# A memory operand gated in other tiles, branch sums moved to VectorE, and a reordered end of an attention stage

## The chip, the cores and the metric

The kernel runs on one core of one Trainium2 chip. A core has TensorE for matrix products (PE in the profile, with PEld for its weight loads), VectorE (DVE), ScalarE (ACT), GpSimd (POOL), and SyncE (SP), whose queue issues most transfers (DMAs) between HBM and the on-chip memory, SBUF. Products land in PSUM, eight banks of 128 x 512 float32. The metric is the time of one execution in microseconds; lower is better.

## The reference, cut to what matters

The kernel computes one encoder block: a normalised input is projected, three mixers run side by side (dilated window attention `oa`, grouped attention `ob`, attention into a fixed memory `om`), each is gated, projected and merged, and one output projection follows.

```python
ya = (oa * jax.nn.silu(ga)) @ w_br_a[layer]
yb = (ob * jax.nn.silu(gb)) @ w_br_b[layer]
ym = (om * jax.nn.silu(gm)) @ w_br_m[layer]
gates = jax.nn.sigmoid((mg + b_merge[layer]).astype(jnp.float32)).astype(dt).reshape(b, s, N_BRANCHES, d)
merged = gates[:, :, 0] * ya + gates[:, :, 1] * yb + gates[:, :, 2] * ym
out = merged @ w_out[layer]
x = x + rms_norm(out, g_post[layer])
```

The sequence has 1024 tokens and the model is 1024 wide; a branch is 512 wide, that is four blocks of 128 channels. Everything is float32: each factor of a product is split into a high part in a reduced format and a low part, and each product is three passes (high x high, high x low, low x high). The helper `split` does it with one ScalarE copy (L105) and one VectorE subtraction (L106).

## The kernel before, in words

All tiles are 128 partitions by 512 or 1024 columns. PE's instructions stand in the order in which the code emits them, and from the value stage on the orders of ACT, DVE, POOL and SP are those of the code too. An engine that waits for one instruction holds back everything behind it; SP's queue does the same with the transfers that it issues.

Three stages matter here.

**The values of head group 0** (the second loop `for n in range(28)`, L1271; PE's line is L1281). Large products are cut in two by two and computed with seven products (Strassen's scheme), `PRODUCTS`: A11, A12, S2, S3, S4, S1, A22. Product i takes the steps n = 4i to 4i+3, twelve 256-column matmuls a step. Its weights must have been summed (`v3_sum`) and split (`v3_split`, into two buffers each of `wh` and `wl`) before step 4i. Results come out through `v3_evac` (DVE additions on L1196) one or two steps after a product's last, and are scaled (ACT L1185, DVE L1183) and stored (SP L1186) by `v3_out`. The dictionary `SIDE` says what else the other engines are given after the matmuls of step n: the splits (S2 at 4, S3 at 8, S4 at 12, S1 at 16, A22 at 20), the token splits `kt_split`, the loads of the next stage's weights (`k_load`), the next stage's first weight sums and splits (`k_sum` on POOL, `k_own` and `k_block` on ACT and DVE, steps 23 to 27), and three strands of interest:

- `operand(r, stage)` (L982) finishes block r of the grouped branch's operand: load its output, its gate and its reciprocals, multiply twice on DVE (L992, L993), store (L995). Stages 1 and 2 of r = 7, the last, stand at steps 2 and 3.
- `memory_operand(k, stage)` (L997) gates block k of the memory branch, 128 x 1024, in two halves: stage 0 loads output and gate into the four half tiles vot, vot, vgt, vrt that `operand` uses too (SP L1003, four transfers of 256 KB), stage 1 multiplies (DVE L1007, twice), stage 2 stores the halves (SP L1011). Block j has its stages at steps 3+3j, 5+3j and 6+3j, none later than 14.
- `tab[0]` and `tab[1]` (L1289) are two 128 x 1024 tiles with the cosines and sines by which the next stage turns queries and keys. They are loaded at step 9 (SP L1258) and multiplied by the row norms at step 11 (`tab[1]`, POOL) and step 17 (`tab[0]`, DVE), both on L1259.

**The query, key, gate and merge products** follow at once (`pair_product`, PE line L1320): for each of 25 pairs the same seven products, in the order A11, A12, S2, S1, S3, A11 of the next pair, A22, and so on. The first needs the tiles of `k_own(0)`, the third, fourth and fifth those of `k_block(0, ...)` for S2, S1 and S3. The merge products' sigmoids, as tanh, go to DRAM (`thd`).

**The window attention with the branch projections beside it** (`weave`, L176, called on L1980). Sixteen items `add_y(m)` (L1864; PE line L1879) are projections of the memory branch (m 0 to 7) and the grouped branch (m 8 to 15), 24 matmuls each in two halves. `weave` alternates them with the steps of the attention by estimated costs: it advances the attention whenever its share of `att_cost` is not above the projections' share. An item puts small jobs on the list `pend`, from which one is taken at every third matmul: `th_load(m+1)` loads the item's gate into one of two wl tiles, `y_load(m+2)` its weights into one of two wr tiles, `y_split(m+1, G)` splits the weights (ACT L1353, POOL L1354), and after each half `y_evac` (L1363). For m below 8 `y_evac` starts the sum `accs`; from 8 on it writes (gate + 1) x product over the gate tile (DVE L1371) and adds that to `accs` (L1372), on POOL below m = 16 and on DVE from there. The last attention pieces come from `ending()` (L1968): small weights are spread over the rows by PE (`wide`), and `first_two(x)` sums two of three terms for column half x. `third(x)` (L1961) adds the third, reading its factor from PSUM, and multiplies by the gate: three DVE operations, L1964 to L1966. `dl_high` (ACT L1859) and `dl_low` (DVE L1862 for block 3) split the result, which is block 3 of the last operand.

After the weave (L1981 on) the code empties `pend`, splits the weights of projections 17 and 18 (`y_split` on ACT L1353 and DVE L1354), loads those of 19 and the first output weights, and then runs `third` and the splits of both halves. The last eight projections (m 16 to 23, PE line L2023) follow: m 16, 17 and 18 first with operand blocks 0 and 1, then with block 2, then with block 3. Their products are tiles of two PSUM banks, three of them, in the place of the weave's six banks. The output products (L2105) end the kernel.

Of the kernel before, what the change touches and what calls it, by code (L numbers as in the profile page):

```python
# [16 lines left out]
NT = 8  # L17
# [33 lines left out]
def block(ctx: ExitStack, tc: tile.TileContext, x, xT, memT, cst, msk, bcst, tabA, gpost,  # L51
# [945 lines left out]
    def memory_operand(k, stage):  # L997

        if stage == 0:
            OT["m"] = [vb.tile([P, 512], F32, name=x, bufs=2 if x == "vot" else 1) for x in ("vot", "vot", "vgt", "vrt")]  # L1000
            for z in range(2):
                for src, dst in ((od, OT["m"][z]), (g2d, OT["m"][2 + z])):
                    nc.sync.dma_start(dst, src[2, k, :, half[z]])  # L1003
        elif stage == 1:
            for z in range(2):
                o, g = OT["m"][z::2]
                V.scalar_tensor_tensor(o, o, 0.5, g, op0=OP.mult, op1=OP.mult)  # L1007
        else:
            o = OT.pop("m")
            for z in range(2):  # L1010
                nc.sync.dma_start(od[2, k, :, half[z]], o[z])  # L1011
# [161 lines left out]
    def v3_split(nm):  # L1173
        h, l = wslot(0), wslot(1)
        split(h, l, V3[nm])
        W3[nm] = [z.rearrange("p (k f) -> p k f", k=4) for z in (h, l)]
# [41 lines left out]
    for n in range(28):  # L1218
# [34 lines left out]
        if k == 3:  # L1253
# [4 lines left out]
            8: [lambda: v3_split("S3")], 9: [lambda: [nc.sync.dma_start(tab[j], tabA[:, j]) for j in range(2)]],  # L1258
            11: [lambda: G.tensor_tensor(tab[1], tab[1], rb, op=OP.mult)], 17: [lambda: V.tensor_tensor(tab[0], tab[0], rb, op=OP.mult)],  # L1259
# [5 lines left out]
    SIDE[2].append(lambda: operand(7, 1))  # L1265
    SIDE.setdefault(3, []).append(lambda: operand(7, 2))
    for j in range(4):
        for z in range(3):
            at = min(3 + 3 * j + (0, 2, 3)[z], 14)
            SIDE.setdefault(at, []).append(lambda j=j, z=z: memory_operand(j, z))  # L1270
# [92 lines left out]
    def y_evac(m, t, ps_):  # L1363
        n, i, f = steps[m]
        th = THS[m]
        if n == 0:
            if accs[f] is None:
                accs[f] = hp.tile([P, S], F32, name=f"acc{f}", tag=f"{('hh', 'hl')[f // 4]}{4 + f % 4}")
            V.scalar_tensor_tensor(accs[f][:, t], th[:, t], 1.0, ps_, op0=OP.add, op1=OP.mult)
        else:  # L1370
            V.scalar_tensor_tensor(th[:, t], th[:, t], 1.0, ps_, op0=OP.add, op1=OP.mult)  # L1371
            (V if m >= 16 else G).tensor_tensor(accs[f][:, t], accs[f][:, t], th[:, t], op=OP.add)  # L1372
# [106 lines left out]
    with ExitStack():  # L1479
# [378 lines left out]
        def dl_high(k, t=slice(0, S)):  # L1858
            A.activation(hh[k][:, t], DL[k][:, t], AF.Copy)  # L1859
# [4 lines left out]
        def add_y(m):  # L1864
            n, i, f = steps[m]

            def gen(_):
                pend.extend([lambda: th_load(m + 1), lambda: y_load(m + 2)])
                if m:
                    pend.append(lambda: y_split(m + 1, G))  # L1870
                if m == 15:
                    pend.append(lambda: y_load(18))
                for t in half:
# [94 lines left out]
        def ending():  # L1968
            DL[3] = C["ogs"][0]
            return [(lambda: [wide(g, 0) for g in range(2)], 500.0), (lambda: [wide(g, 1) for g in range(2)], 500.0),  # L1970
                    (lambda: [first_two(0), wide(2, 0)], 2500.0), (lambda: [first_two(1), wide(2, 1)], 2500.0)]
# [8 lines left out]
        weave(16, every(), FIRST_PAD + 12 * NT * (SOFT + 100.0) + 4 * LAST_PAD + 8000.0)  # L1980
        while pend:  # L1981
            pend.pop(0)()
        y_split(17)
        y_split(18, V, qk.tile([P, S], R, name="aq", bufs=2))
# [5 lines left out]
        third(0)  # L1990
        dl_high(3, lo)
        third(1)
        dl_low(3, lo)
        dl_high(3, hi)
        dl_low(3, hi)
# [340 lines left out]
```

## Time and profile before

| what | us |
|---|---|
| median of 3 runs | 1445.68 |
| lowest, highest | 1442.84, 1447.82 |
| the profiled execution's own time | 1446.26 |
| its span, first to last instruction | 1444.5 |

The profiled execution lies 0.58 us above the median, and 1.76 us of it lie around the span. The page lists, engine by engine, busy time, a strip of 40 slices with the TensorE clock that was granted, the chain of work that ended last, and the costliest groups of instructions. Views of the trace behind it give the instructions in order of time (start, duration, engine, line, operands, and in brackets the idle time before and what ended it), who waited for whom, and busy times by stretch. Times in them count from the span's start.

### The profile page before, as it was taken

The numbers are of one execution on the slowest core, as the hardware profiler recorded it, in microseconds if no ns is written. First come the engines' busy times: TensorE is split into PE (matmuls) and PEld (weight loads), VectorE is DVE, ScalarE is ACT, GpSimd is POOL, SyncE is SP. The second block draws the span as 40 slices with busy tenths as digits, with TensorE's granted clock in tenths as the row PEclk, the third lists the DMA queues.
The fourth block names the chain that finished last, engine by engine and source line by source line (L and its number), as shares of the span: only waits on it lengthen the run. The fifth ranks groups of instructions, "written<-read, shape, count | busy, mean of one in ns | idle before, by whom it ended". The sixth has DMA issues, their size and how long they took to land.

```text
span 1444.5 us, 21871 instructions
## 1 busy us (share of the span) xinstructions
PE 1392.9 (96%) x7775; PEld 1112.6 (77%) x7775; DVE 1012.0 (70%) x1811; ACT 659.6 (46%) x1384; POOL 596.2 (41%) x457
## 2 busy tenths in 40 slices
PE   8999999999999996799999999999999999998997
PEld 7799986666666886788888888888887777676886
DVE  7768578776763883667787776677776556556977
ACT  6544356665644442233333333333345665552332
POOL 1416703666664000244555554455541154572003
PEclk9999999999999998899999999999999999999999
DMA  6356432222111887614233333333356666755555
GB/s 237 96 169 227 168 121 88 96 77 95 60 48 49 278 277 218 196 69 143 81 111 117 113 108 116 105 114 117 117 159 204 198 191 210 237 143 175 172 206 175
DMA packets 122013, 212.30 MB, mean 147 GB/s; under 512 B 32592, under 2 KB 61104, under 8 KB 121904
## 3 DMA queue, kind: packets, MB, share of 16 engines
q1 hardware_dynamic: 112112, 196.88, 42.7%
q10 hardware_dynamic: 9792, 14.03, 2.7%
q8 instruction: 61, 1.00, 0.3%
q14 instruction: 48, 0.39, 0.1%
HBM read 144.48 MB, written 66.38 MB: 146 GB/s over the span
## 4 chain that ended last, share of the span: by engine, by line
PE 80%; DMA 6%; DVE 4%; POOL 3%; ACT 3%; issue 3%; SPq 1%; ACTq 0%; DVEq 0%; POOLq 0%
PE s L1320 33%; PE s L2105 4%; PE d L1879 4%; PE s L1226 4%; PE ov L797 3%; PE sc L2023 3%; PE d L145 3%; PE d L143 3%; PE d L147 3%; PE s L782 2%; PE s L781 2%; PE tr L763 2%; PE d L2105 2%; PE s L1580 1%; PE tr L1652 1%
## 5 line engine op out<-in xcount | busy, mean ns | idle before, releaser
L788 POOL TENSOR_TENSOR bl<-bl,bp 128x512 f32<-128x512 f32 x96 | 130.8, 1362 | 54.3 <-ACT bp L784 48.9
L1320 PE MATMUL s<-hh,vS 128*128 128x512 f32 x400 | 133.4, 395 | 0.0
L1320 PE MATMUL s<-vA,vS 128*128 128x512 f32 x450 | 106.6, 390 | 0.0
L106 DVE TENSOR_TENSOR vS<-vot,vS 128x512 fp32r<-128x512 f32 x75 | 86.3, 1152 | 20.2 <-ACT vS L105 20.2
L1320 PEld LDWEIGHTS s<-vA,vS 128*128 128x128 f32 x450 | 84.5, 188 | 18.3
L1593 ACT ACTIVATE pra<-pra,sts 128x192 f32<-128x192 f32 (+2 forms) x176 | 75.3, 429 | 46.9 <-DVE sts L1592 39.5
L784 ACT ACTIVATE bp<-s 128x512 f32<-128x512 f32 x128 | 75.7, 595 | 43.7 <-PE s L782 42.8
L764 DVE TENSOR_REDUCE bn<-tr 128x1 f32<-128x512 f32 x128 | 84.8, 683 | 12.2 <-PE tr L763 11.0
L143 PE MATMUL d<-hh,wh 128*128 128x512 f32 x224 | 90.0, 402 | 2.4 <-DVE fth L216 2.4
L147 PE MATMUL d<-hh,wl 128*128 128x512 f32 x224 | 90.2, 403 | 0.0
L145 PE MATMUL d<-hl,wh 128*128 128x512 f32 x224 | 89.5, 400 | 0.0
L1320 PEld LDWEIGHTS s<-hh,vS 128*128 128x128 f32 x400 | 75.3, 188 | 17.7
L1320 PE MATMUL s<-hl,vS 128*128 128x512 f32 x200 | 79.1, 395 | 0.0
L1320 PE MATMUL s<-hh,wh 128*128 128x512 f32 x200 | 78.4, 392 | 0.0
L1320 PE MATMUL s<-hh,wl 128*128 128x512 f32 x200 | 78.4, 392 | 0.0
L1320 PE MATMUL s<-hl,wh 128*128 128x512 f32 x200 | 77.8, 389 | 0.0
L1631 DVE COPY app<-tr 128x384 f32<-128x384 f32 (+1 forms) x64 | 38.8, 606 | 46.5 <-PE tr L1619 29.7
L1324 ACT ACTIVATE vv<-s 128x512 f32<-128x512 f32 x50 | 29.9, 598 | 85.2 <-PE s L1320 58.7
L797 PE MATMUL ov<-bp,VS 128*64 128x512 f32 x256 | 58.5, 599 | 0.0
L1060 POOL TENSOR_TENSOR vot<-vot,vA 128x512 f32<-128x512 f32 x12 | 19.3, 1609 | 90.8 <-DVE vS L106 90.8
L143 PEld LDWEIGHTS d<-hh,wh 128*128 128x128 f32 x224 | 42.6, 190 | 16.3 <-issue 5.5
L1592 DVE CUSTOM_DVE_ANT_0 pra<-s,mask 128x192 f32<-128x192 f32 (+2 forms) x192 | 53.9, 323 | 1.1 <-PE s L1580 1.1
(621 smaller groups left out, 4077.9 us busy)
## 6 DMA issues: line engine op xcount, KB each, us to landing
wr<-in_wu SPq DMA_DIRECT2D x40, 512.0 KB
vA<-in_wu SPq DMA_DIRECT2D x24, 512.0 KB
qkd<-ko SPq DMA_DIRECT2D x96, 128.0 KB
wl<-thd SPq DMA_DIRECT2D x24, 512.0 KB
wos<-os SPq DMA_DIRECT2D x12, 512.0 KB
wr<-in_wbr SPq DMA_DIRECT2D x24, 256.0 KB
aq<-qkd SPq DMA_DIRECT2D x12, 512.0 KB
ak<-qkd SPq DMA_DIRECT2D x12, 512.0 KB
```

The source lines that it names most:

```text
L106: V.tensor_tensor(dst_l, src, dst_h.bitcast(F32), op=OP.subtract)
L143: PE.matmul(dst, wh[:, k, :], hh[k][:, t], start=k == 0, stop=False)
L145: PE.matmul(dst, wh[:, k, :], hl[k][:, t], start=False, stop=False)
L147: PE.matmul(dst, wl[:, k, :], hh[k][:, t], start=False, stop=k == 7)
L764: fp["last"] = V.tensor_reduce(st[i]["n"][:, j, c:c + 1], s, axis=AX.X, op=OP.min)
L784: A.activation(pp, s, AF.Exp, scale=-1.0)
L788: G.tensor_tensor(lsum[i % 2], lsum[i % 2], pp, op=OP.add)
L797: PE.matmul(o[e * 64:e * 64 + 64], VS[:, kt, kv], d.pop(kt), start=kt < 2, stop=kt >= NT - 2)
L1226: PE.matmul(now[j], a, b, start=k == 0 and q == 0, stop=k == 3 and q == 2)
L1320: PE.matmul(BANK[n, c], a, b, start=k == 0 and q == 0 and not more, stop=k == 3 and q == 2, skip_group_check=c in "XW")
L1593: A.activation(src, src, AF.Exp, scale=-1.0, bias=bias, accum_out=sts[:, h, 1, T:T + 1])
L2105: PE.matmul(dst[:, e[0]:e[1]], a, b, start=k == 0 and q == 0, stop=k == 3 and q == 2)
```

## The change

It has four parts.

1. `memory_operand` takes whole blocks through `tab[0]` and `tab[1]`, two 512 KB loads, one 1024-wide multiplication, one 512 KB store, in two stages: the load at step 2+5j, the multiplication and the store at step 6+5j. The tables are loaded at step 22, after the last block, and both are multiplied by DVE, `tab[1]` at step 26 and `tab[0]` at step 27. Stages 1 and 2 of `operand(7)` move to step 7.
2. `y_evac` writes (gate + 1) x product back into the product's PSUM bank, and DVE adds it from there, for all m from 8 on.
3. In `add_y`, `th_load(m+1)` comes after `y_load(m+2)`, `y_split(m+1)` and, for m = 15, `y_load(18)`.
4. `third(0)` and `dl_high(3, lo)` become a last piece of `ending()`, and `att_cost` grows by that piece's 2500. After the weave, `third(1)` and the splits of block 3 stand before `y_split(17)`, between it and `y_split(18)`, and no longer after the output weights' loads.

```diff
     def memory_operand(k, stage):
         if stage == 0:
-            OT["m"] = [vb.tile([P, 512], F32, name=x, bufs=2 if x == "vot" else 1) for x in ("vot", "vot", "vgt", "vrt")]
-            for z in range(2):
-                for src, dst in ((od, OT["m"][z]), (g2d, OT["m"][2 + z])):
-                    nc.sync.dma_start(dst, src[2, k, :, half[z]])
-        elif stage == 1:
-            for z in range(2):
-                o, g = OT["m"][z::2]
-                V.scalar_tensor_tensor(o, o, 0.5, g, op0=OP.mult, op1=OP.mult)
+            nc.sync.dma_start(tab[0], od[2, k])
+            nc.sync.dma_start(tab[1], g2d[2, k])
         else:
-            o = OT.pop("m")
-            for z in range(2):
-                nc.sync.dma_start(od[2, k, :, half[z]], o[z])
+            V.scalar_tensor_tensor(tab[0], tab[0], 0.5, tab[1], op0=OP.mult, op1=OP.mult)
+            nc.sync.dma_start(od[2, k], tab[0])
...
-            8: [lambda: v3_split("S3")], 9: [lambda: [nc.sync.dma_start(tab[j], tabA[:, j]) for j in range(2)]],
-            11: [lambda: G.tensor_tensor(tab[1], tab[1], rb, op=OP.mult)], 17: [lambda: V.tensor_tensor(tab[0], tab[0], rb, op=OP.mult)],
+            7: [lambda: operand(7, 1), lambda: operand(7, 2)], 8: [lambda: v3_split("S3")],
...
-    SIDE[2].append(lambda: operand(7, 1))
-    SIDE.setdefault(3, []).append(lambda: operand(7, 2))
     for j in range(4):
-        for z in range(3):
-            at = min(3 + 3 * j + (0, 2, 3)[z], 14)
-            SIDE.setdefault(at, []).append(lambda j=j, z=z: memory_operand(j, z))
+        for z in range(2):
+            SIDE.setdefault(2 + 5 * j + 4 * z, []).append(lambda j=j, z=z: memory_operand(j, z))
+    SIDE[22].append(lambda: [nc.sync.dma_start(tab[j], tabA[:, j]) for j in range(2)])
+    for j in range(2):
+        SIDE[26 + j].append(lambda j=j: V.tensor_tensor(tab[1 - j], tab[1 - j], rb, op=OP.mult))
...
-            V.scalar_tensor_tensor(th[:, t], th[:, t], 1.0, ps_, op0=OP.add, op1=OP.mult)
-            (V if m >= 16 else G).tensor_tensor(accs[f][:, t], accs[f][:, t], th[:, t], op=OP.add)
+            V.scalar_tensor_tensor(ps_, th[:, t], 1.0, ps_, op0=OP.add, op1=OP.mult)
+            V.tensor_tensor(accs[f][:, t], ps_, accs[f][:, t], op=OP.add)
...
-                pend.extend([lambda: th_load(m + 1), lambda: y_load(m + 2)])
+                pend.append(lambda: y_load(m + 2))
                 if m:
                     pend.append(lambda: y_split(m + 1, G))
                 if m == 15:
                     pend.append(lambda: y_load(18))
+                pend.append(lambda: th_load(m + 1))
...
-                    (lambda: [first_two(0), wide(2, 0)], 2500.0), (lambda: [first_two(1), wide(2, 1)], 2500.0)]
+                    (lambda: [first_two(0), wide(2, 0)], 2500.0), (lambda: [first_two(1), wide(2, 1)], 2500.0),
+                    (lambda: [third(0), dl_high(3, lo)], 2500.0)]
...
-        weave(16, every(), FIRST_PAD + 12 * NT * (SOFT + 100.0) + 4 * LAST_PAD + 8000.0)
+        weave(16, every(), FIRST_PAD + 12 * NT * (SOFT + 100.0) + 4 * LAST_PAD + 10500.0)
         while pend:
             pend.pop(0)()
+        third(1)
+        dl_high(3, hi)
+        dl_low(3, lo)
         y_split(17)
+        dl_low(3, hi)
         y_split(18, V, qk.tile([P, S], R, name="aq", bufs=2))
         y_load(19)
...
-        third(0)
-        dl_high(3, lo)
-        third(1)
-        dl_low(3, lo)
-        dl_high(3, hi)
-        dl_low(3, hi)
```

## The prediction

> **What bounds the kernel now.** First the page's busy table and clock strip, then a view of busy times cut at the stage borders (stretch and its length, busy time and instructions of PE, PEld, DVE, ACT and POOL, granted clock, share of the DMA engines, GB/s).
>
> ```profile
> PE 1392.9 (96%) x7775; PEld 1112.6 (77%) x7775; DVE 1012.0 (70%) x1811; ACT 659.6 (46%) x1384; POOL 596.2 (41%) x457
> PEclk9999999999999998899999999999999999999999
> ```
> ```profile
> 538.90:605.50 66.60, 46.64 (x339) 45.54 (x338) 34.77 (x47) 17.38 (x28) 6.25 (x4) 0.85 0.71 220
> 605.50:1083.00 477.50, 477.50 (x2076) 390.26 (x2076) 350.17 (x379) 175.43 (x277) 243.71 (x146) 1.00 0.36 113
> 1083.00:1306.40 223.40, 217.63 (x2036) 165.84 (x2036) 133.01 (x551) 130.54 (x463) 103.97 (x57) 1.00 0.64 195
> 1306.40:1359.60 53.20, 46.82 (x194) 37.80 (x194) 39.79 (x51) 16.80 (x30) 3.32 (x3) 0.94 0.61 203
> ```
>
> PE is the bound nearly everywhere: 96% busy, and without a gap in the pair products (second row). Two stages leave it idle at a lowered clock (0.85 and 0.94), and the change works in both: the group-0 values (first row) and the last projections (fourth). What PE waited for:
>
> ```profile
> 562.32 0.53 PE L1281 MATMUL s<-wh,vA 128*128 128x256 f32 x2 [4.64 <-ACT wh L105]
> 585.14 0.58 PE L1281 MATMUL s<-wl,hh 128*128 128x256 f32 x1 [12.99 <-DVE wl L106]
> ...
> 605.19 0.28 PE L1281 MATMUL s<-wl,hh 128*128 128x256 f32 x1
> 605.31 0.40 PE L1320 MATMUL s<-hh,wh 128*128 128x512 f32 x1
> ...
> 1315.17 0.77 PE L2023 MATMUL sc<-hh,wh 128*128 128x512 f32 x1 [5.78 <-ACT hh L1859]
> ```
> ```profile
> PE d L143 <- DVE fth L216: 2.4, 1, 2.4
> PE d L1879 <- POOL wh L1354: 1.5, 1, 1.5
> ```
>
> The value stage runs from 538.9 to 605.3, 66.4 us. At full clock its matmuls start 0.12 us apart (605.19 to 605.31); 7 x 4 x 12 = 336 of them are 40.3 us, so 26 us are lost. Who held the weights back is in DVE's and SP's orders of time:
>
> ```profile
> 556.07 0.69 DVE L1007 SCALAR_TENSOR_TENSOR vot<-vot,vgt 128x512 f32<-128x512 f32 x1 [3.61 <-DMA vgt<-g2d]
> 580.63 0.69 DVE L1007 SCALAR_TENSOR_TENSOR vot<-vot,vgt 128x512 f32<-128x512 f32 x1 [11.59 <-DMA vgt<-g2d]
> 583.87 1.22 DVE L106 TENSOR_TENSOR wl<-wr,wh 128x1024 fp32r<-128x1024 f32 x1
> ```
> ```profile
> 546.83 2.71 SPq L953 DMA_DIRECT2D vdr<-vy  x4
> 551.95 0.62 SPq L1003 DMA_DIRECT2D vgt<-g2d  x1
> 562.01 7.39 SPq L1186 DMA_DIRECT2D vdr<-vv  x4
> 569.44 1.00 SPq L1258 DMA_DIRECT2D tab<-in_tabA  x2
> 570.48 0.91 SPq L1011 DMA_DIRECT2D od<-vot  x2
> 576.51 0.32 SPq L1003 DMA_DIRECT2D vot<-od  x1
> ```
>
> DVE stood 11.59 us before the third block's gating, and the split that PE wanted (583.87) was queued behind it. The gating waited for loads at 576.51, these for the stores at 570.48 to leave the half tiles, and those were issued late behind value stores (562.01 to 569.40) and the table loads. The loop store, load, multiply ends last here, with DVE in the middle.
>
> **Part 1, the gating.** Removed: eight half multiplications, sixteen loads and eight stores. Added: four multiplications of 1024 columns (1.22 us, the size of the row at 583.87), eight loads and four stores of 512 KB, on one pair of buffers instead of four half tiles. The loop stays, one per block and longer, as the halves no longer overlap. Durations from the chain of work:
>
> ```profile
> 139.64 2.92 DMA wos<-os
> ...
> 570.48 6.01 DMA od<-vot
> ...
> 577.82 4.65 DMA vrt<-g2d
> ...
> 583.38 2.06 DMA od<-vot
> ...
> 585.83 5.62 DMA vrt<-g2d
> ```
>
> A 512 KB store has no row in this place; between 2.06 (half of it) and 6.01 (two halves behind the tables) I take 2.92, a 512 KB store elsewhere. Loading both tiles: 1 MB asked for from 583.38 on had landed at 591.45, with a wait between, and the last pieces of a megabyte took 4.65 and 5.62; I take 5.62, ends 4.65 and 8. A round is 2.92 + 5.62 + 1.22 + 0.45 for the issue = 10.2 us, ends 8.4 and 15.7.
>
> SP reaches the first loads after its value stores, at 549.6. In before the first half pair, out at 551.95 + 0.62, let DVE start at 556.07; the double bytes, sooner, give about 557.0, so block 0 is gated at 558.2. `operand(7)`'s two multiplications and S3's split follow, and PE, which wants S3 at 556.4, waits until about 562 as before. From there PE needs 16 steps of 12 x 0.12 us and some 2.5 us for the half clock after the wait, to about 587.7. S4 and A22 are split while DVE waits for nothing longer; S1's split stands ahead of block 2 at step 16. Block 3 is gated at 558.2 + 3 x 10.2 = 588.8, and `k_own(0)` stands behind it:
>
> ```profile
> 599.77 0.91 ACT L1185 ACTIVATE vy<-vy,rcol 128x256 f32<-128x256 f32 x2 [5.71 <-DVE vy L1196]
> 600.59 1.05 ACT L105 ACTIVATE wh<-wr 128x1024 fp32r<-128x1024 f32 x1
> ```
>
> Two 512-wide additions (0.6 each, half of the 1.22 above), scaling (0.9), ACT's copy (1.05) and most of DVE's 1.22 put the first pair product at about 593.0 instead of 605.3: **-12.3**. What is late next: PE waits some 4 us before it. The store and tables after block 3 (2.92 + 5.62 + 0.45) land at 597.8; DVE stands there with `k_block` S1 and S3 queued behind `tab[1]`'s 1.22, done at 599.7; PE wants S1 three products after 593.0, at 601.2: a product is 12 of the 25 x 7 x 12 matmuls that fill the 477.5 us of the second row, 2.73 us. This costs nothing by 1.5 us. POOL loses a 2.34 us multiplication that nothing waits for.
>
> The clock. In the same cut view, two short stretches:
>
> ```profile
> 54.00:57.00 3.00, 3.00 (x9) 2.34 (x8) 3.00 (x5) 0.58 (x2) 1.92 (x3) 0.51 0.79 242
> ...
> 1315.00:1318.00 3.00, 2.83 (x7) 2.29 (x8) 2.83 (x6) 1.58 (x4) 0.00 (x0) 0.50 0.95 294
> ```
>
> Half clock follows the wait of 2.4 us on L143 (first row) and that of 5.78 (second), and the value stage's 4.64 and 12.99 stand behind its 0.85; the wait of 1.5 left its stage at 1.00. I charge the new wait before the pair products 3.4 us at half clock, **+1.7** (ends 0 and +3.4). [...]
>
> **Part 2, the sums.** Sixteen POOL additions (m 8 to 15) go; DVE gets sixteen more.
>
> ```profile
> L1371 DVE SCALAR_TENSOR_TENSOR wl<-wl,d x16: 673/677/689, 1207.9 to 1307.2; 128x512 f32<-128x512 f32 x16
> ```
> ```profile
> L1372 POOL TENSOR_TENSOR acc<-acc,wl x16: 1259/1282/1735, 1208.6 to 1308.4; 128x512 f32<-128x512 f32 x16
> L1372 DVE TENSOR_TENSOR acc<-acc,wl x8: 1224/1226/1227, 1332.0 to 1360.9; 128x1024 f32<-128x1024 f32 x8
> ```
>
> A write to PSUM in this form has no row; the nearest read PSUM at 0.677 and the SBUF sum is 1.226 for twice the columns, so I take 0.68 for each new addition, ends 0.61 and 1.2: 16 x 0.68 = 10.9 us more of DVE, 20.5 less of POOL. DVE is 60% busy in that stage, so nearly all of it lies beside PE; it delays softmax steps PE waits for now and then: **+0.5**, ends -1.9 (POOL's additions no longer stretch DVE's own, as part 4's 2.98 against 1.13) and +4 (a third of it on the path). The product's bank is held 0.7 us longer, of two; PE waited for none of them before. For m from 16 on DVE's work is the same in count and width: 0.
>
> **Part 3, the loads.** SP stood at `th_load(15)` and `th_load(16)` until POOL's late additions freed the gate tiles, with the weight loads behind. This is the tail of SP's order, and what came of it:
>
> ```profile
> 1298.98 0.33 SPq L1361 DMA_DIRECT2D wl<-thd  x1
> ...
> 1305.96 6.17 SPq L1348 DMA_DIRECT2D wr<-in_wbr  x3
> ```
> ```profile
> 1307.25 0.67 DVE L1371 SCALAR_TENSOR_TENSOR wl<-wl,d 128x512 f32<-128x512 f32 x1
> 1311.07 0.69 DVE L1354 TENSOR_TENSOR wh<-wr,wh 128x512 fp32r<-128x512 f32 x1 [3.15 <-ACT wh L1353]
> ...
> 1314.34 0.68 DVE L1964 TENSOR_TENSOR og<-tr,og 128x512 f32<-128x512 f32 x1
> ```
>
> With weights first, `y_load(17)` leaves at about 1300.4 and is no longer the limit. POOL, 20.5 us lighter, should split item weights sooner, and the 1.5 us wait on L1354 goes: **-1.5**, ends 0 and -1.5. The gates, later by two small jobs, are needed an item later.
>
> **Part 4, the third term.**
>
> ```profile
> L1959 DVE TENSOR_TENSOR og<-og x2: 1127/2052/2978, 1301.4 to 1306.2; 128x512 f32<-128x512 f32 x2
> ```
>
> PE's 5.78 us wait ended at 1315.17, just after `third(1)` had read PSUM (1314.34 + 0.68): the second product tile takes banks of the weave, so that read is the gate, not the ACT copy the row names. Without the wait for weights DVE becomes the limit. It begins the second half of `first_two` at 1302.5, since the sum at 1301.4 should take the shorter of that row's two times, 1.13, with POOL's additions gone. Then, at 0.68 to 0.69 an operation (1307.25, 1311.07 and 1314.34): two multiplications 1.3, the sum 1.13, `y_evac(15)` first half 1.37, `third(0)` 2.06, second half 1.37, `third(1)` 2.06, `dl_low` 0.68, split 0.69: 10.6 us, to 1313.1, with ACT's part of the split 0.6 earlier. PE, done with m 16 at 1309.4, starts near 1312.9: **-2.2**, ends 0 and -5.8. [...]
>
> **The sum**: -12.3 + 1.7 + 0.5 - 1.5 - 2.2 - 0.9 = -14.7 against 1446.26: 1431.6; the median shown is 0.58 lower, so **1431**.
>
> **Rivals.**
> - Quick rounds (8.4): block 3 gated at 583.4, so PE ends at its own 588 with `k_own` done: -17.5, and no low clock; with the tail's wait gone too, -17.5 - 1.5 - 5.8 - 2.6 + 0.5 = -27: 1419. For it: single stores of 2.06. Against: 1 MB loads are slow in all rows. 12%.
> - Full clock after both new waits, if some 4 us are too short for the drop: 1.7 twice is not paid, 1428. For it: the wait of 1.5 left the clock whole, and the drops of both stages stand behind 4.64 and more; against: the one after 2.4. [...] 15%.
> - Slow rounds (12, store and loads a fifth longer) and a tail unchanged, since `third(1)` gates PE still: part 1 is -12.3 + 3 x 1.8 + 1.7 = -5.2, the rest -1.0: 1439.5. For it: two `k_load`s run beside block 3's loads. 17%.
> - The change doesn't do what it says: the rounds are as slow as before's 576.51 to 591.45 (14.9), so part 1 gives back its 12.3, and the tail alone is left: within 0.3%, 1442 to 1446. 6%.
> - Slower: the tables are now the fifth round, ahead of `k_block` S1 on DVE. S1 is then ready at 558.2 + 4 rounds + 0.7; before, PE wanted it at 605.3 + 8.2 = 613.5. With -4.1 of the tail it decides from a round of 14.7 us; at 15.7 S1 comes 8.2 us later than in before; with +1.7 of clock, the tail's -4.1 and DVE's other end (+3.5) that is 1455. Against it: it takes the slowest row each time. 6%.
> - The forecast: 44%.
>
> **How the numbers follow.** Range 1420 to 1441: it leaves out a little of the quick case and the last two. A measurement here tells 0.3%, 4.3 us, from no change. Faster by more than that: 44 + 12 + 15 + 17 = 88%; same 6%, slower 6%.
>
> **What would show it.** `memory_operand`'s multiplications some 10 us apart, the last near 588; the first L1320 near 593; a PE wait of about 4 us before it, on DVE or ACT; no POOL on L1372 and sixteen DVE rows there near 0.68; PE's first wait on L2023 near 3.5 us. Wrong if DVE reaches block 3 after 595, if PE waits at the pair product with S1, or if PE's idle time between 1200 and 1306 grows by over 2 us.

## The result, and the profile after

| kernel | median, us | lowest to highest | profiled execution: time, span |
|---|---|---|---|
| before | 1446.4 (6 runs) | 1442.84 to 1449.24 | 1446.26, 1444.5 |
| after | 1438.27 (6 runs) | 1435.44 to 1440.64 | 1439.34, 1437.5 |

The ratio is 0.9942, with a 95% interval of 0.9923 to 0.9961: faster by 0.58%, where 14.7 us, 1.0%, were forecast. The sign and the range held; nearly half of the gain is missing. Of the page, the busy table and the clock strip:

```profile
PE 1395.1 (97%) x7775; PEld 1113.6 (77%) x7775; DVE 1023.4 (71%) x1824; ACT 659.1 (46%) x1384; POOL 573.1 (40%) x440
PEclk9999999999999999999999999999999999998999
```

The two 8s of before, in slices 16 and 17 (the value stage), are gone; the one 8 of after, in slice 37, is in the last projections. But PE is busy 2.2 us longer than before on the same 7775 matmuls, so clock was lost elsewhere. The cut view at after's stage borders (value stage, pair products, weave, last projections; columns as in the prediction) says where:

```profile
538.10:587.40 49.30, 42.73 (x338) 41.99 (x336) 29.99 (x37) 16.15 (x25) 1.65 (x2) 0.93 0.76 259
587.40:1079.40 492.00, 486.72 (x2101) 396.93 (x2102) 361.83 (x391) 180.21 (x285) 247.65 (x148) 0.99 0.38 118
1079.40:1298.00 218.60, 213.71 (x2012) 163.33 (x2011) 136.13 (x561) 126.92 (x459) 85.40 (x42) 0.99 0.65 195
1298.00:1352.20 54.20, 47.85 (x193) 38.51 (x192) 40.77 (x53) 16.96 (x30) 0.00 (x0) 0.91 0.52 180
```

The pair products and the weave stood at 1.00 before and now stand at 0.99; the last projections fell from 0.94 to 0.91. To compare kernels exactly I take the time from a stage's first matmul to the next stage's first (the last column is when the value stage begins):

| kernel | value | pair products | weave | last projections | output | begins | span |
|---|---|---|---|---|---|---|---|
| before | 66.2 | 483.3 | 217.8 | 53.0 | 85.1 | 539.1 | 1444.5 |
| after | 49.1 | 492.0 | 218.7 | 54.2 | 85.3 | 538.3 | 1437.5 |
| difference | -17.1 | +8.6 | +0.9 | +1.2 | +0.2 | -0.8 | -6.9 |

So the value stage gained 17 us and half of that was given back at once, in a stage that had run without a gap. PE's order of time, at the waits that matter:

```profile
561.56 0.80 PE L1273 MATMUL s<-wh,vA 128*128 128x256 f32 x2 [5.83 <-ACT wh L105]
...
587.43 0.50 PE L1312 MATMUL s<-hh,wh 128*128 128x512 f32 x1 [0.30 <-ACT wh L105]
...
590.73 0.80 PE L1312 MATMUL s<-hh,wl 128*128 128x512 f32 x1 [2.57 <-DVE wl L106]
...
601.42 0.96 PE L1312 MATMUL s<-aq,vS 128*128 128x512 f32 x3 [2.68 <-ACT vv L1316]
...
1202.85 0.70 PE L1572 MATMUL s<-ak,aq 64*128 64x128 f32 x4 [1.55 <-DVE sts L1584]
...
1305.44 0.80 PE L2015 MATMUL sc<-hh,wh 128*128 128x512 f32 x1 [4.48 <-ACT wh L1345]
...
1323.31 0.52 PE L2015 MATMUL sc<-hh,wh 128*128 128x512 f32 x1 [1.87 <-DVE acc L1364]
```

The 12.99 us wait of before is gone, and the first pair product starts at 587.43 instead of 605.31. New are the two waits at 590.73 and 601.42, the one of 1.55 in the weave, and the one of 1.87 where before waited 0.60. Behind the waits at 590.73, 1202.85, 1305.44 and 1323.31 stands a lowered clock. The same cut view on four short stretches of after:

```profile
589.70:596.50 6.80, 5.77 (x14) 4.53 (x15) 6.00 (x9) 2.47 (x5) 1.28 (x1) 0.50 0.98 284
1204.20:1207.50 3.30, 3.30 (x17) 2.57 (x18) 1.78 (x9) 2.00 (x9) 0.00 (x0) 0.50 0.27 83
1303.20:1309.90 6.70, 4.46 (x11) 3.46 (x12) 3.47 (x6) 1.92 (x4) 0.00 (x0) 0.50 0.42 129
1323.60:1327.00 3.40, 3.40 (x9) 2.63 (x8) 3.37 (x5) 0.00 (x0) 0.00 (x0) 0.50 0.68 263
```

Half of PE's busy time in each is lost: 2.9 us in the pair products, 1.7 in the weave, 2.2 and 1.7 in the last projections. With the waits, 2.57 + 2.68 + 2.9 = 8.2 of the pair products' 8.6 us are accounted for (the 0.30 at 587.43 lies ahead of their first matmul).

**Where the gating stands now.** The first and the last of DVE's four multiplications (start, duration, and in brackets how long DVE stood for the loads):

```profile
556.42 1.23 DVE L1003 SCALAR_TENSOR_TENSOR tab<-tab,tab 128x1024 f32<-128x1024 f32 x1 [7.13 <-DMA tab<-g2d]
...
583.66 1.23 DVE L1003 SCALAR_TENSOR_TENSOR tab<-tab,tab 128x1024 f32<-128x1024 f32 x1 [4.80 <-DMA tab<-g2d]
```

Three rounds lie between them, 27.24 us, so 9.1 us a round, where the forecast had 10.2. **And what came after them**, the chain of work that ends at the product S2 (start, length, what):

```profile
583.66 1.24 DVE tab L1003
...
584.91 3.04 DMA od<-tab
...
588.39 5.56 DMA tab<-in_tabA
...
593.98 1.93 DVE tab L1262
595.90 1.21 DVE vS L106 x2
597.11 2.23 DVE tab L1262
599.34 0.61 DVE vy L1189
...
600.39 0.49 ACT vy L1178
600.88 0.49 ACT vv L1316
...
601.42 0.73 PE s L1312 x2
```

Block 3's store must leave `tab[0]` before the tables come, the tables land at 593.95, DVE multiplies them, and only then evacuates the last value product (L1189). ACT scales that (L1178) and copies the pair product's bank behind it (`keep_copy`, L1316), and PE cannot begin S2 before that bank is copied. For the store and the loads behind block 3 the forecast took 2.92 and 5.62, and they measured 3.04 and 5.56; the splits that it watched were never late.

### The profile page after: what moved, and what is told of

Same layout as the page of the kernel before. It is cut to its first block, busy times and chain, and to the rows that moved or that the text cites. A ratio compares the mean times of both kernels' runs of the same rounds, so it can differ in the third digit from the quotient of the medians.

```text
span 1437.5 us, 21813 instructions
## 1 busy us (share of the span) xinstructions
PE 1395.1 (97%) x7775; PEld 1113.6 (77%) x7775; DVE 1023.4 (71%) x1824; ACT 659.1 (46%) x1384; POOL 573.1 (40%) x440
## 4 chain that ended last, share of the span: by engine, by line
PE 52%; DMA 4%; DVE 3%; SPq 1%; POOL 1%; issue 1%; ACT 0%; ACTq 0%; DVEq 0%; POOLq 0%
PE s L1312 33%; PE d L1872 4%; PE s L2097 4%; PE sc L2015 3%; PE s L1572 2%; PE d L2097 2%; PE tr L1644 1%; DMA tab<-g2d 1%; DMA avs<-vdr 1%; PE tr L1611 1%; DMA od<-tab 1%; PE tr L1620 1%; PE tr L1637 1%; DVE acc L1364 0%; DMA tab<-in_tabA 0%
## 5 line engine op out<-in xcount | busy, mean ns | idle before, releaser
L788 POOL TENSOR_TENSOR bl<-bl,bp 128x512 f32<-128x512 f32 x96 | 130.5, 1360 | 54.3 <-ACT bp L784 48.9
L1053 POOL TENSOR_TENSOR vot<-wr 128x512 f32<-128x512 f32 x13 | 22.2, 1709 | 127.0 <-DMA vA<-in_wu 127.0
L1316 ACT ACTIVATE vv<-s 128x512 f32<-128x512 f32 x50 | 29.9, 598 | 85.1 <-PE s L1312 58.6
```

Of the source, the lines that this page charges most:

```text
L788: G.tensor_tensor(lsum[i % 2], lsum[i % 2], pp, op=OP.add)
```

## The experiments

Twelve kernels. Lines are those of each kernel. Ratios are to the kernel before, run on the same chip, with 95% intervals; after's is 0.9942.

### 1. Part 1 alone, and parts 2 to 4 alone

The kernel before with after's `memory_operand`, table loads and step list; and the kernel after with before's.

> The kernel before with part 1 alone (gating through the tables' tiles, tables loaded and multiplied last, operand 7 at step 7). The changed kernel's trace has a value stage that is 17.0 us shorter and pair products that are 8.6 us longer. Theory: both belong to part 1, the second as three debts of its longer chain (a 2.6 us wait for the first pair's split, a 2.7 us wait at the pair product S2, and half clock after them). Then this run has both, the value stage near 49 us and the pair products near 492 us, its span 8 to 10 us under the kernel before, and the median as much: about 1437. Rival: the loss in the pair products comes with the other parts or by chance of that execution; then the pair products take about 483.5 us here and the span is 16 to 17 us under the kernel before.

Measured: 1440.36 us, ratio 0.9954 (0.9939 to 0.997); value stage 48.2, pair products 492.7. The gain and its loss are both part 1's own; PE's waits by what ended them (us in all, times, longest):

```profile
PE d L1871 <- POOL wh L1346: 3.1, 2, 2.8
PE s L1312 <- ACT vv L1316: 3.1, 1, 3.1
PE s L1312 <- DVE wl L106: 2.9, 1, 2.9
```

The second and third rows are after's two waits again. The first is the wait on POOL's weight split that the forecast had part 3 remove, here 2.8 us long and with a half clock behind it: the weave of this kernel takes 221.0 us, 3.2 more than before's, and so the span is only 6.2 us under before's where the theory had 8 to 10.

> The kernel before with parts 2, 3 and 4 and without part 1. Theory: the parts behind the pair products bring nothing and cost 1 to 3 us: weave 217.8 to about 218.7 us, last projections 53.0 to about 54.2 us, so the median is 1 to 3 us above the kernel before, within what a measurement tells. Rival (the prediction's own sum): they bring 4 us, 1442, and what the changed kernel lost there came only from a different phase of the clock after its earlier start.

Measured: 1445.2 us, ratio 0.9982 (0.997 to 0.9994), span 1443.4: weave 217.7 (before 217.8) and last projections 54.3 (before 53.0). Neither expectation is met, and the three parts together bring next to nothing. They hold a gain and a loss, as the runs below show. The two halves of the change, 0.46% and 0.18%, add up to about after's 0.58%.

### 2. The waits at the pair products: one late thing or two

```diff
-            23: [lambda: k_sum(0, 1)], 24: [lambda: k_own(0)], ...
+            23: [lambda: k_sum(0, 1)], 21: [lambda: k_own(0)], ...
```

> The kernel after, with k_own(0) three steps sooner, so that DVE splits it ahead of block 3's gating (DVE stands idle 4.80 us there) and not behind it beside POOL's sums. Theory, that two waits stand in a row in front of one late thing (ACT's keep_copy behind DVE's multiplication of the tables, done at 600.79): the wait of 2.57 us at 590.73 and the half clock behind it go, but PE then stands that much longer ahead of product S2, some 5 to 8 us instead of 2.68; pair products from their first matmul 490 to 493 us as in the kernel after (491.95), time within 0.1% of it. Rival, that each wait costs for itself: 2.57 and 2.9 us of clock are won, pair products 486.5, time 0.35% lower than after.

Measured: 1438.9 us, ratio 0.9942 (0.9919 to 0.9964), the same as after. The 2.57 us wait is gone, and PE stands at S2 instead:

```profile
601.37 1.22 PE L1312 MATMUL s<-aq,vS 128*128 128x512 f32 x2 [8.72 <-ACT vv L1316]
```

S2 starts at 601.37, against 601.42 in after: the theory's point, a wait taken away in front of a later one is only moved. Pair products took 495.1 us, 2 over the theory's upper bound, because the half clock was moved too: it now stands behind the wait ahead of S2 (granted clock 0.50 from 601.30 to 607.50), where its 3.1 us delay everything that follows, and in after it lay ahead of S2. The wait and the clock, 8.72 + 3.1, are what lies between before's 483.3 and these 495.1.

The other way round, the tables' multiplications behind the eviction and the copy:

```diff
-    for j in range(2):
-        SIDE[26 + j].append(lambda j=j: V.tensor_tensor(tab[1 - j], tab[1 - j], rb, op=OP.mult))
...
     keep_copy(p1, 0)
+    for j in range(2):
+        V.tensor_tensor(tab[1 - j], tab[1 - j], rb, op=OP.mult)
```

> The kernel after, with the two multiplications of the turning tables moved on DVE behind keep_copy(p1,0) and its eviction. Theory: DVE's eviction of A22 no longer stands behind them, ACT's copy is done sooner, and the wait of 2.68 us ahead of product S2 goes; the wait of 2.57 us at the pair product's second weights stays. Pair products 489 us against 491.95, span some 2.5 to 3 lower than after's 1437.5. Rival, that POOL's sums hold ACT's copy or that k_block's S1 and S3 are late for themselves: the wait stays at 2 to 3 us or moves to the next product, span within 1 us of after.

Measured: 1434.03 us, ratio 0.9903 (0.9876 to 0.9929), span 1433.5, pair products 489.05. S2's row has no wait; the one at the low weights, 2.79 us, stays:

```profile
598.29 0.86 PE L1310 MATMUL s<-aq,vS 128*128 128x512 f32 x3
```

It starts 3.1 us sooner, the pair products are 2.9 us shorter, and the span 4.1, somewhat more than expected: the theory holds, and the two multiplications on DVE, in front of an eviction that ACT's copy waits for, are shown as the cause of the 2.68.

### 3. The gating spread over the stage

```diff
-        for z in range(2):
-            SIDE.setdefault(2 + 5 * j + 4 * z, []).append(lambda j=j, z=z: memory_operand(j, z))
-    SIDE[22].append(lambda: [nc.sync.dma_start(tab[j], tabA[:, j]) for j in range(2)])
+        SIDE.setdefault((2, 9, 17, 22)[j], []).append(lambda j=j: memory_operand(j, 0))
+        if j < 3:
+            SIDE.setdefault((8, 16, 21)[j], []).append(lambda j=j: memory_operand(j, 1))
...
     keep_copy(p1, 0)
+    memory_operand(3, 1)
+    for j in range(2):
+        nc.sync.dma_start(tab[j], tabA[:, j])
...
+        if n == 0:
+            for j in range(2):
+                V.tensor_tensor(tab[1 - j], tab[1 - j], rb, op=OP.mult)
         c_fin(n, 0, 0)
```

`k_own(0)` is at step 21 here too.

> The kernel after with the blocks' gating spread: loads at steps 2, 9, 17, 22, gatings at step 8 behind S3's split, 16 behind S1's split and 21 behind k_own(0); block 3's gating, its store and the tables' loads behind keep_copy(p1,0), the tables' multiplications just ahead of the first c_fin. So no split of weights stands behind a gating whose loads are late. Theory, that PE's weights were late only by their place behind the loop in DVE's order: the value stage falls from 49.1 to 42 to 44 us, the waits of 2.57 and 2.68 us and the half clock of 590 go, pair products 484 to 486; span 1437.5 less 10 to 13 us. Rival, that the loop itself ends last wherever it stands: the first c_fin then waits for the tables, the pair products take 490 or more, and the span falls by under 5 us.

Measured: 1425.63 us, ratio 0.9835 (0.9798 to 0.9872), span 1424.6. The cut view from the value stage's first matmul to the pair products' first, and on to the weave's:

```profile
538.96:579.46 40.50, 40.43 (x337) 40.22 (x336) 29.24 (x35) 15.56 (x23) 1.04 (x1) 1.00 0.82 269
579.46:1066.32 486.86, 483.56 (x2102) 394.93 (x2101) 360.40 (x392) 180.27 (x285) 247.36 (x149) 1.00 0.38 123
```

The value stage is within 0.2 us of the 40.3 that its 336 matmuls need, below the theory's 42 to 44, at full clock: even the S3 wait of 4.6 to 5.8 us, which the forecast had left in place, was gating ahead of a split in DVE's order. The pair products miss the theory's 484 to 486 by 0.9:

```profile
588.38 0.50 PE L1310 MATMUL s<-aq,vS 128*128 128x512 f32 x1 [3.29 <-ACT vv L1314]
```

The same copy is late again, now with no table in front of it: DVE has the splits of `k_block` S2, S1 and S3 ahead of the eviction. Experiment 7 moves those of S1 and S3 behind it.

### 4. The sums: PSUM held, and DVE's sixteen additions

From m 16 on, the first operation writes to the gate's SBUF tile as in before:

```diff
-            V.scalar_tensor_tensor(ps_, th[:, t], 1.0, ps_, op0=OP.add, op1=OP.mult)
-            V.tensor_tensor(accs[f][:, t], ps_, accs[f][:, t], op=OP.add)
+            x = th[:, t] if m >= 16 else ps_
+            V.scalar_tensor_tensor(x, th[:, t], 1.0, ps_, op0=OP.add, op1=OP.mult)
+            V.tensor_tensor(accs[f][:, t], x, accs[f][:, t], op=OP.add)
```

> The changed kernel, but for projections 16 to 23 the product times the gate is written to the gate's tile in SBUF as before, so that a PSUM tile is free after the first of the two DVE operations and not after the second. DVE's work is the same. Theory: PE's 1.87 us wait at the first matmul of projection 19 is for the PSUM tile of projection 16, which the new form holds 1.22 us longer; then the wait falls to about 0.6 us, the half clock of 3.4 us after it goes, and the last projections take 2 to 3 us less (about 51.5 us). Rival: DVE is simply late there because its tail is longer; then the wait stays at 1.9 us.

Measured: 1435.75 us, ratio 0.9914 (0.9896 to 0.9932), last projections 50.8 against 54.2. The wait of 1.87 us is back at before's size, and ends with the first operation and not with the sum. Of the 3.4 us, 1.3 are that wait and 1.7 the half clock behind it:

```profile
1317.85 0.47 PE L2016 MATMUL sc<-hh,wh 128*128 128x512 f32 x1 [0.60 <-DVE wl L1364]
```

Now the sums of m 8 to 15 on POOL again (`x = ps_ if m >= 16 else th[:, t]`, the addition on POOL below 16):

> The kernel after, with the sums of m 8 to 15 on POOL again, by way of the gates' SBUF tile as in the kernel before; m 16 on as in after. Theory, that the sixteen additions cost DVE little more than their place beside PE: the weave stays within 1 us of 218.65, and a wait on POOL's L1354 split comes back (1.5 us) while the one of 1.55 us on DVE's softmax sum at 1202.85 goes. Rival, that the additions on DVE are what spoilt part 3's gain: the weave falls by 2 to 4 us, to 215 to 216.5.

Measured: 1435.02 us, ratio 0.9912 (0.9883 to 0.994), weave 214.0. My theory falls and the rival holds, with a fall of 4.6 us where it had 2 to 4: the additions on DVE did cost. Holding the product's bank longer is not what cost here, for in after's weave no wait of PE stands on L1872, the line of these products. The cut view over exactly the weave, to be held against the third row of after's:

```profile
1081.64:1295.67 214.03, 211.31 (x2012) 161.53 (x2011) 127.36 (x549) 127.00 (x459) 103.86 (x57) 1.00 0.66 197
```

PE stands 4.9 us in after and 2.7 here (length less busy time), DVE is 8.8 us busier in after, and PE itself works 2.4 us longer there, most of it the half clock behind the wait of 1.55 us on DVE's softmax sums; that wait is 0.78 here. POOL's L1354 wait does not come back.

Both undone together:

> The kernel after without any of part 2: the products are added through the gates' SBUF tiles again, m 8 to 15 on POOL, m 16 on by DVE; parts 1, 3 and 4 stay. Theory, that the two costs of part 2 add up (weave 218.65 to 214.03 when POOL takes m 8 to 15, last projections 54.20 to 50.82 when the product's PSUM tile is released by the first operation): weave 213 to 215, last projections 50 to 51.5, no wait of 1.87 us near 1318, span 1437.5 less 7 to 9 us. Rival, that both gain from the same clock and the same late gate: the span stays at the 1430.5 to 1432.1 of the two halves, under 7 us below after.

Measured: 1434.93 us, ratio 0.991 (0.9895 to 0.9925), span 1434.0; last projections 50.1 as the theory has it, but weave 216.6 and pair products 493.7, so neither expectation is met. The code of the pair products is after's; there S2 starts at 602.2, where the tables let it, whose loads took 7.0 us here and 5.56 in after. Of the weave's 2.6 us over the run before, 2.0 lie in small waits on ACT and on DMAs, and why they fall so is left open. Taken over all runs the weave is 216.3 to 218.9 us in the seven with DVE's additions and part 3 (mean 217.6), 213.9 to 216.6 in the five with POOL's and part 3 (mean 214.7): part 2 costs it 2.9 us, with a scatter of about 1.3 on each side. Part of the 2.9 is half clock: 1.7 us in after (0.50 at 1204.20:1207.50), and none in the run with POOL's sums above (weave at 1.00).

### 5. Parts 3 and 4 without part 2

> The kernel before with parts 3 and 4 alone: gating and sums as in before. Theory, that part 2 took back what parts 3 and 4 bring (the three together: weave 217.67, last projections 54.33, span 1443.4): weave 214 to 216.6, without a wait on L1354 and without half clock, last projections 50 to 51 with a first wait of 3.5 us; span 1444.5 less 3 to 5.5 us. The prediction's own terms for them, -1.5, -2.2 and -0.9, say 4.6 less. Rival, that parts 3 and 4 bring nothing without part 1's shift of the weave: weave 217 or more, span within 1.5 us of before.

Measured: 1439.47 us, ratio 0.9954 (0.9938 to 0.997), span 1435.2; weave 213.9, last projections 49.6. PE's waits from the weave on, of this kernel and then of the one with part 2 added:

```profile
PE sc L2023 <- ACT wh L1353: 3.4, 1, 3.4
PE s L1580 <- DVE sts L1592: 1.2, 3, 0.8
...
PE sc L2023 <- DVE wl L1371: 0.6, 1, 0.6
```

```profile
PE sc L2023 <- ACT wh L1353: 4.5, 1, 4.5
PE s L1580 <- DVE sts L1592: 1.9, 3, 1.5
PE sc L2023 <- DVE acc L1372: 1.9, 1, 1.9
```

Row by row part 2 adds 1.1 us in front of the last projections, 0.7 on the softmax sums and 1.3 on the product tile, and its stages are 3.8 and 4.8 us longer. Most of the rest is half clock: the granted clock was 0.99 against 1.00 in the weave, 0.91 against 0.97 in the last projections. The theory holds, with a little more than it expected of both stages: parts 3 and 4 bring 3.9 us in the weave and 3.4 in the last projections, and part 2 takes them back. The rest of the 9.2 us between the two spans lies ahead of the weave, in code that is before's own: the value stage begins 0.7 us sooner and is 1.3 us shorter. That is a difference between two executions, and the medians, 6.7 us apart by the ratio, hold less of it.

### 6. The first wait of the last projections

```diff
-        third(1)
-        dl_high(3, hi)
-        dl_low(3, lo)
         y_split(17)
+        third(1)
+        dl_high(3, hi)
+        dl_low(3, lo)
```

> The changed kernel with the split of projection 17's weights put ahead of third(1), as the first thing after the weave. Theory: PE's 4.48 us wait on the last projections is for ScalarE's half of that split, which stands behind the copy of the second half of block 3, and this behind third(1) on DVE; put first, the wait ends with third(1)'s read of PSUM, at about 2.7 us, and its row names DVE and third. The last projections take 1.5 to 3 us less. Rival: third(1)'s read of PSUM is the gate in the changed kernel as well, and the split was ready by then; putting the split first delays third(1) by 0.7 us and the wait grows to about 5 us.

Measured: 1433.42 us, ratio 0.9897 (0.9879 to 0.9916); last projections 48.75 at full clock. The stage is 5.5 us shorter than in after, where the theory had 1.5 to 3: about 2 us are the first wait, and the rest is half clock (2.2 and 1.7 us in after), absent here. The gate is now `third(1)`'s read of PSUM, as the forecast read it in before's trace:

```profile
1302.93 0.47 PE L2015 MATMUL sc<-hh,wh 128*128 128x512 f32 x1 [2.53 <-DVE og L1957]
...
1318.91 0.47 PE L2015 MATMUL sc<-hh,wh 128*128 128x512 f32 x1 [1.87 <-DVE acc L1364]
```

The second wait is as long as in after. That the clock behind it is 1.00 (1318.90:1322.30), where after has 0.50, is not counted as this edit's gain: what decides it was not shown (last section).

### 7. A version from what was found

Gating spread as in 3, `k_block` S1 and S3 behind `keep_copy(p1, 0)`, sums as in before, and `y_split(17)` first. Of the edit, the part that is new:

```diff
-            26: [lambda: k_block(0, "S2")], 27: [lambda: k_block(0, "S1"), lambda: k_block(0, "S3"), lambda: k_sum(0, 4)]}
+            26: [lambda: k_block(0, "S2")], 27: [lambda: k_sum(0, 4)]}
...
     keep_copy(p1, 0)
+    k_block(0, "S1")
+    k_block(0, "S3")
+    memory_operand(3, 1)
```

> Gating spread as in gates_spread, with k_block S1 and S3 moved on DVE and ACT behind keep_copy(p1,0); sums as in the kernel before; y_split(17) ahead of third(1). Theory: each gain stands in another stage and they add: value stage 40.5, pair products 483 to 485 (the wait of 3.3 us ahead of product S2 falls below 1.5), weave 214 to 216, last projections 47 to 49; span 1437.5 less 20 to 24 us, 1414 to 1418. Rival, that a change of the weave's start shifts its plan and a wait with half clock comes back (as the weave of 220.98 with part 1 alone): span 1418 to 1424.

Measured: **1412.88 us** (1412.48 to 1416.01), ratio 0.9761 (0.9746 to 0.9777): 2.4% under before, 1.8% under after. The four stages, value to last projections:

```profile
538.61:579.57 40.96, 40.43 (x337) 40.21 (x336) 29.03 (x36) 15.57 (x23) 0.81 (x1) 1.00 0.79 261
579.57:1064.63 485.06, 483.97 (x2102) 394.77 (x2101) 361.21 (x391) 180.19 (x285) 248.68 (x149) 1.00 0.38 123
1064.63:1278.67 214.04, 211.55 (x2012) 161.88 (x2011) 128.31 (x549) 126.92 (x459) 103.87 (x57) 1.00 0.65 197
1278.67:1325.79 47.12, 44.28 (x193) 35.81 (x192) 39.57 (x49) 16.97 (x30) 1.92 (x2) 1.00 0.61 217
```

All four have the full clock; the wait ahead of S2 is 0.60 us. The span, 1411.4, is under the theory's 1414 to 1418, each stage at or next to its forecast.

The last one puts only the operation of `third(1)` that reads PSUM ahead of `y_split(17)`, and both ahead of the emptying of `pend`:

```diff
+        third(1, 0)
+        y_split(17)
         while pend:
             pend.pop(0)()
-        y_split(17)
-        third(1)
+        third(1, 1)
```

> As spread_split_sums, but in the tail only the operation of third(1) that reads PSUM stands ahead of y_split(17), the rest of third(1) behind it. Theory: PE's first wait in the last projections, which third's read of PSUM ended when the split came first, falls from 2.5 to about 1 us, last projections 46 to 47.5. Rival, that the read waits on PE's own late W3 gates: the wait stays at 2 us or more and the stage at 48 to 49.

Measured: 1414.74 us, ratio 0.977 (0.9756 to 0.9783), not to be told from the one above. PE's first wait fell from 2.24 to 0.24 us, but one of 1.50 us follows it, on ACT's split of projection 18's weights: again a wait is mostly moved. The stage took 47.4 us (47.1 above), so its forecast of 46 to 47.5 was met and nothing was won.

## Why the prediction was right in sign and half in size

The forecast was 7.7 us under the profiled execution (1431.6 against 1439.34). By its terms:

| | forecast | profiled | |
|---|---|---|---|
| part 1 with its clock | -10.6 | -9.3 | value stage, its begin, pair products |
| parts 2 and 3 in the weave | -1.0 | +0.9 | |
| part 4, its clock, m from 16 | -3.1 | +1.2 | |
| output | 0 | +0.2 | |

**The loop, right.** The rounds came out at 9.1 us instead of 10.2, between the quick end of 8.4 and the value taken, and block 3 was gated at 583.66 + 1.23 = 584.9 and not at 588.8. Its consequence, `k_own(0)` behind it and the pair product's low weights late, came too, but with some luck. The wait is on the split of `k_own`, 2.57 us long instead of some 4; it stands at the third matmul, on DVE's low weights, and not before the first, and it ended at 590.73, only 2.3 us sooner than forecast, though block 3 was gated 3.9 us sooner. DVE's work between ran slow beside POOL's sums (rows below), for which the forecast had no term.

**The tables: "This costs nothing by 1.5 us" failed.** The forecast followed what stands behind `tab[1]` on DVE only as far as the splits of `k_block`, done at 599.7 against a need at 601.2. Behind the multiplications on DVE stood also the eviction of A22, behind that on ACT the scaling and `keep_copy`, and behind that PE. It cost 2.68 us, and the half clock that the forecast had at 1.7 was 2.9. The multiplications took 1.93 and 2.31 us and not 1.22: POOL was at its sums for `k_sum` beside them.

```profile
588.29 1.30 POOL L1053 TENSOR_TENSOR vgt<-wr 128x512 f32<-128x512 f32 x1
593.54 1.28 POOL L1053 TENSOR_TENSOR vot<-wr,vot 128x512 f32<-128x512 f32 x1 [3.95 <-DVE vS L106]
596.59 1.67 POOL L1053 TENSOR_TENSOR vot<-vA 128x512 f32<-128x512 f32 x1 [1.76 <-DVE vS L106]
598.22 2.25 POOL L1053 TENSOR_TENSOR vgt<-vA,vA 128x512 f32<-128x512 f32 x1
```

```profile
586.12 2.36 DVE L1176 TENSOR_SCALAR vv<-vv,rcol 128x256 f32<-128x256 f32 x2
588.39 2.28 DVE L106 TENSOR_TENSOR wl<-wr,wh 128x1024 fp32r<-128x1024 f32 x1
...
597.03 2.31 DVE L1262 TENSOR_TENSOR tab<-tab,rb 128x1024 f32<-128x1024 f32 x1
```

The second DVE row is the split that ended the wait of 2.57, also stretched from 1.22, and the two scalings in the first took 0.61 at 591.91, with POOL idle: together 2.8 us, about the whole of that wait. No run takes POOL's sums away from there, so this is read from the rows and not shown by an experiment. By these rows the split and the two tables each end 1.1 us after the end of the POOL addition that began before them (589.59, 594.82 and 598.26), and POOL's last addition, 2.25 us in place of 1.28, ends 1.1 us after the second table.

**Part 2: +0.5 was 4 to 6.** By the ratios it costs 0.32% (after against sums_as_before) and 0.28% (parts234_only against parts34_only), 4.6 and 4.1 us; by the stages of the profiles, below, 3.4 + 2.9, half clock included. Two steps failed. "For m from 16 on DVE's work is the same in count and width: 0" counted work and not how long PSUM is held: the tile of projection 16 is free only after the sum, PE waits 1.87 instead of 0.60, and in after a half clock follows; undone alone, the stage is 3.4 us shorter. And the sixteen additions, each at the forecast's size,

```profile
L1364 DVE TENSOR_TENSOR acc<-d,acc x16: 691/692/692, 1201.8 to 1301.5; 128x512 f32<-128x512 f32 x16
```

cost the weave 2.9 us on the mean, within the ends of -1.9 and +4 but far from the value taken: a stage in which DVE is 60% busy on average still has PE waiting for DVE at the softmax sums.

**Part 3: right in kind, too small.** -1.5 was the wait on L1354, which went. Against before the weave without part 2 is 3.1 us shorter on the mean, 3.9 in the run of parts 3 and 4. More went with it than that wait. That the loads' order did this, and not part 4's piece in the weave's plan, was not tried apart. In after the weave is 0.9 us longer than before all the same: PE stands 4.9 us in it, not 5.8, but 1.7 are lost to half clock, where before lost none.

**Part 4: right, and covered by part 2.** PE "starts near 1312.9", 6.5 us into the stage; it was 7.4 (1305.44, from 1298.03), with a wait of 4.48 and not 3.5. The forecast's chain on DVE, from the second half of `first_two` to the split of projection 17, came out: 10.4 us to PE's start (1302.5 to 1312.9), and 10.0 in after (1295.43 to 1305.44). But it began 2.6 us ahead of the stage's first matmul, not 3.9; why is left open. Without part 2 (experiment 5) PE started 6.4 us into the stage, after a wait of 3.44, and the stage was 3.4 us shorter than before, against the -3.1 of part 4; one difference offsets another there, for its sums take 1.3 us beside POOL's, and DVE has none of the additions of m 8 to 15. In after the wait on the product tile, 1.3 us more than before's, and 1.7 us of half clock behind it take that back. No run shows the -0.9 of the sum, for less half clock in this stage, apart from the rest, nor the quick rival's -2.6, which is all that before lost there (0.50 over the 5.24 us from 1315.17): the granted clock of the last projections was 0.94 in before, 0.97 in experiment 5 and 0.91 in after. The forecast summed the order as it found it: `y_split(17)` behind the whole of `third(1)`, its ACT copy behind `dl_high(3, hi)`. That the order itself cost was not asked; experiment 6 shows it.

**The rivals.** Slow rounds came nearest in time (1439.5), but for a reason that is wrong: rounds were quicker than forecast, and of the tail it said that nothing is won there, which came true for another reason: part 2's cost, and not `third(1)`. The rival at full clock was wrong: 0.50 stands behind the new waits at 590.73 and 1305.44.

## What to carry to other kernels

Follow a late instruction through every engine's queue to the next thing that PE needs, evictions and copies included, and not only through the engine where it stands: a wait that is removed in front of another late thing is moved, not won, and what pays is the order in the queues. When a result is kept in PSUM for one more operation, count how long the bank is held, and who wants it, before the engine's work. An engine that is 60% busy on average has no free places where another engine waits for it.

## What the runs showed of the hardware

The clock's drop did not go by a wait's length alone. In gates_spread a wait of 3.29 us (588.38) stands in a stage with full clock: the pair products, 486.86 us long, take 483.6 without it, and before's, without a gap, 483.3. In after a wait of 1.55 us (1202.85) has 0.50 behind it (1204.20:1207.50).

Nor did the same wait have the same clock behind it in two kernels. The wait of 1.87 us on the product tile has 0.50 behind it in after (1323.60:1327.00); in experiment 6 it has a full clock:

```profile
1318.90:1322.30 3.40, 3.39 (x15) 2.83 (x16) 3.37 (x5) 0.00 (x0) 0.00 (x0) 1.00 0.78 284
```

So a wait of this length cost 1.7 us more in one kernel and nothing more in another. What decides it was not shown: these are readings of traces, and no experiment moved a wait and left the rest alone.
